# Gate matrix of a PEER layer: one-hot rows laid out for four tokens side by side instead of eight

## Chip, cores and metric

One core of a Trainium2 chip. The metric is the device time of one execution in microseconds, from the runs of the kernel; the profile is of one execution of the same program. TensorE (PE in the rows, its weight loads PEld) multiplies matrices, VectorE (DVE), ScalarE (ACT) and GpSimd (POOL) work on elements, SyncE (SP) issues most loads.

## What is computed

A diffusion backbone layer: two parallel token mixers on 1024 latent and 256 context tokens, then a PEER feed-forward part with 16384 experts of one neuron each. Only the second part is touched here. Cut to that:

```
q = (tok @ wq).reshape(-1, 8, 2, 128)
s1 = einsum("nhd,kd->nhk", q[:, :, 0], k1);  s2 = einsum("nhd,kd->nhk", q[:, :, 1], k2)
v1, i1 = top_k(s1, 16);  v2, i2 = top_k(s2, 16)
top_s, top_c = top_k((v1[..., :, None] + v2[..., None, :]).reshape(-1, 8, 256), 16)
expert = i1[top_c // 16] * 128 + i2[top_c % 16];  gate = softmax(top_s)
act = gelu(einsum("pd,ped->pe", xb, u[expert]))
out = einsum("pe,ped->pd", gate * act, v[expert])
```

Each token has 8 heads with 16 chosen experts each, so 128 slots: a first key, a second key (0 to 127 each) and a gate.

## The kernel before

The mixers come first, then norm, keys and the choice of experts. For the first 256 tokens (two blocks of 128) the rows of the chosen experts are gathered. The other 768 tokens go through all 128 expert tiles of 128 experts, and what a token has not chosen gets a gate of zero. For this a gate matrix is needed: for each token a 128 x 128 matrix over (first key, second key), with the gates at the chosen places.

`gate_block` (line 995) makes it for 32 tokens at a time. `turn` (985) has put the slots on the partitions: `rT[slot, j, token]` with the first key, the second key, and the gate as two fp16 halves that add up. `iota` holds 0 to 127, each repeated for `TB` tokens. For `TB` = 8 tokens VectorE makes the tile `oh` of shape [slot, 4, key, token] in four operations (lines 1002 to 1005): one-hot rows of the first key, one-hot rows of the second key, and these times each half of the gate. The token is the innermost dimension, so the 128 key values of one token lie 8 fp16 values, 16 bytes, apart. Then TensorE multiplies for each token the one-hot rows of the first key by the two gated rows of the second key, summed in PSUM (line 1010): the stationary operand is `oh[:, 0, :, t]` and the moving one `oh[:, 2 or 3, :, t]`, both read at that step. Four tokens (8 matmuls of 128 columns) fill one PSUM tile `pgm`, of which there is one buffer (tag `go`), and ScalarE evicts it into `gs` (line 1012). After 32 tokens `gs` is stored to `G_d`.

Six blocks of 128 tokens make 192 such groups of 8 matmuls: two blocks first, then the choice for the second half of the tokens, then four blocks. `prep` strings these steps together as a generator that yields an estimated time. For each `U_US` = 10.5 of it one early expert tile is put in: `u_turn` (transposes `put`, line 913, and the split of `uT`) and `u_act` (48 matmuls `ph` by the helper at line 99, evicted as `ac`), and two gather steps (line 892, and the product at 871 on VectorE). The framework's scheduler then settles the order of the instructions on each engine. `choosing` (scores `psc`, queries `pq`, top 16 on VectorE) and `route` (line 945 on) run between them too. All later expert tiles follow in a stage of their own, where the matmuls `pe` sum four tiles at a time.

Of the kernel before, what the change touches and what calls it, by code (L numbers as in the profile page):

```python
# [18 lines left out]
P = 128  # L19
# [12 lines left out]
# powers of two that keep the low halves of split operands out of fp16's subnormals  # L32
# [11 lines left out]
NB = 32          # tokens in a block of the gate matrix  # L44
TB = 8           # tokens whose one-hot rows are made at once
GR = 4           # expert tiles summed in PSUM at once
NGB = 2          # blocks of 128 tokens whose experts' rows are gathered
T0 = NGB * P     # the other tokens go through every expert
# [18 lines left out]
def tile_layer(ctx: ExitStack, tc: tile.TileContext, x, c, ctxt, c_ctx, ada_w, ada_b, norm_mix_g,  # L67
# [22 lines left out]
    def split(src, hi, lo, scale):  # L90
        """hi + lo = scale * src, each in fp16"""
        S.activation(hi, src, AF.Copy, scale=float(scale))  # L92
        return V.scalar_tensor_tensor(out=lo, in0=src, scalar=float(scale), in1=hi, op0=ALU.mult, op1=ALU.subtract)  # L93
# [32 lines left out]
    # activations by feature: the mixers' input first, the experts' input later  # L126
# [5 lines left out]
    def rms_cols(tiles, pl, tag):  # L132
        """1 / rms of each row of the tiles"""
        n = len(tiles)
        ss = pl.tile([P, n], F32, name=f"ss_{tag}", tag="ss", bufs=3)
        for i, t in enumerate(tiles):
            sq = pl.tile([P, D], F32, name=f"sq_{tag}{i}", tag="sq")
            S.activation(sq, t, AF.Square, accum_out=ss[:, i:i + 1])
        S.activation(ss, ss, AF.Ln, scale=1.0 / D, bias=eps)
        S.activation(ss, ss, AF.Exp, scale=-0.5)  # L140
        return ss

    def norm_T(tiles, ss, dst, sc, sh, pl, pp, tag, rows_of=None):
        """normalised rows, by feature, with a gain and a shift per feature, split in two"""
        for i, t in enumerate(tiles):
            tsc(V, t, t, ss[:, i:i + 1], ALU.mult)
        w = len(tiles) * P
        for k in range(KC):
            pt = pp.tile([P, 512], F32, name=f"pt_{tag}{k}", tag="pt", bufs=2)
            for i, t in enumerate(tiles):  # L150
                PE.transpose(pt[:, i * P:(i + 1) * P], t[:, k * P:(k + 1) * P], ident)
            hi = dst(0, k)
            S.activation(hi, pt[:, :w], AF.Identity, scale=sc(k), bias=sh(k))
            yt = pl.tile([P, 512], F32, name=f"yt_{tag}{k}", tag="yt", bufs=2)
            tsc(V, yt[:, :w], pt[:, :w], sc(k), ALU.mult, sh(k), ALU.add)
            tt(G, dst(1, k), yt[:, :w], hi, ALU.subtract)
            if rows_of is not None:
                rows_of(k, yt)
# [4 lines left out]
    # ================================================================ mixers  # L163
    with ExitStack() as mixers:
        def slab(src, c0, nm, sc, pool_lo=False):
            """128 columns of a weight, split"""
            w32 = ws.tile([P, KC, P], F32, name=f"w32_{nm}", tag="w32", bufs=3)
            ld(out=w32, in_=src[:, c0:c0 + P].rearrange("(k p) c -> p k c", p=P))
            w16 = ws.tile([P, 2, KC, P], F16, name=f"w16_{nm}", tag="w16", bufs=3)
            if pool_lo:  # L170
                tsc(G, w32, w32, float(sc), ALU.mult)
                S.copy(w16[:, 0], w32)
                tt(G, w16[:, 1], w32, w16[:, 0], ALU.subtract)
            else:
                split(w32, w16[:, 0], w16[:, 1], sc)
            return w16
# [5 lines left out]
        # ---------------------------------------------------------- modulation and norm  # L182
        with ExitStack() as sa:
# [40 lines left out]
            # lower bounds: softmax over the two layers, first entry: 1/2 + 1/2 tanh of half the difference;  # L224
            # columns: (1 + lb) / 2, (1 - lb) / 2, -(1 - lb) / 2
# [10 lines left out]
            # normalised rows by feature  # L236
# [56 lines left out]
        # tokens in three ranges: context, first half, second half  # L293
# [5 lines left out]
        def proj(w16, r, nm, pp, m=P):  # L299
            """128 columns of a projection by feature, for one range of tokens"""  # L300
            ps = pp.tile([P, 512], F32, name=f"pj_{nm}_{r}", tag="pj", bufs=2)
            o = ps[:m, :LEN[r]]
            mm3(o, lambda k: w16[:, 0, k, :], lambda k: w16[:, 1, k, :], lambda k: SRC[r][:, 0, k, :], lambda k: SRC[r][:, 1, k, :])
            return o
# [5 lines left out]
        # masks over a pair of chunks: [s, c] is kept where s and c share a chunk and s precedes c in scan order  # L310
# [18 lines left out]
        # scans restart at each chunk: zeros at the chunks' first tokens, one column early for the backward direction  # L329
# [5 lines left out]
        def v_natural(c0, nm):  # L335
            """256 value columns by token"""
# [17 lines left out]
        def gates_of(d, lf, kt, qt, esc, nm):  # L354
            """cumulates the log gates in place; queries and keys in each chunk's frame, keys by token, entry decays"""
# [49 lines left out]
        def chains(sds, v, vs, nm):  # L405
            """r[direction][position]: the state that enters a chunk, before its entry decay"""
# [30 lines left out]
        def outputs(hf, v, vs, sds, rs_, nm):  # L437
            """o by token for half of the tokens and 128 value channels, both directions"""
            po = pq.tile([P, 512], F32, name=f"o_{nm}_{hf}", tag="o", bufs=2)
            for d in range(2):  # L440
                for i in range(4):
                    p_ = hf * 4 + i
                    PE.matmul(po[:, i * P:(i + 1) * P], lhsT=scT[d][:, p_, :], rhs=v[:, 2 + p_, vs],
                              start=d == 0 and i == 0, stop=False)
            for i in range(4):
                for d in range(2):
                    for j in range(2):
                        ci = 2 * (hf * 4 + i) + j
                        PE.matmul(po[j * CH:(j + 1) * CH, i * P:(i + 1) * P], lhsT=sds[d][0][:, ci * CH:(ci + 1) * CH],
                                  rhs=rs_[d][:, ci, :], start=False, stop=i == 3 and d == 1)  # L450
            return po
# [7 lines left out]
        def head_out(v, sds, gates, gcs, ydst, nm):  # L459
            """states, outputs, head norm and gate"""  # L460
# [45 lines left out]
        def gate_tile(c0, nm):  # L506
            """z (1 + tanh(z / 2)) = 2 silu(z), up to the projection's scale"""
# [103 lines left out]
        def merge_gate(u):  # L611
            """tanh of half a merge gate, for 128 channels, kept in DRAM"""
# [8 lines left out]
        def modulation(j):  # L621
            """shift, scale or gate number j of the latent tokens: sums over the rows of ada_w, 128 of them at a time"""
# [61 lines left out]
        # ---------------------------------------------------------- merge, output projection, first half's keys  # L684
# [11 lines left out]
        def scores(hf, h, ps_pool):  # L696
            """scores of 512 tokens against both sets of keys, for one head"""
# [23 lines left out]
        def choose(hf, h, s_all, i):  # L721
            """top 16 of each key set, then of their 256 sums, for 128 tokens and one head"""
# [18 lines left out]
        def choosing(hf, ps_pool, then=None):  # L741
            """one head of half of the tokens at a time"""
# [68 lines left out]
        def h2_rows(k, yt):  # L811
            """the gathering tokens' h2 by token"""
# [43 lines left out]
    # ================================================================ PEER  # L856
# [7 lines left out]
    def gathering():  # L864
        """the chosen experts of the first tokens, a row per token at a time; rows are used AHEAD steps after their load"""
# [41 lines left out]
    def u_turn(e, un, early):  # L907
        """u of the experts i * 128 + e by feature, i on the free axis, split"""
# [16 lines left out]
    def u_act(e, uT):  # L925
        """gelu(u . h) of those experts for every token"""
# [9 lines left out]
    # product keys, gates and the gate matrix; expert tiles with e % GR == 0 go first meanwhile  # L936
    with ExitStack() as st:
# [7 lines left out]
        def route(n):  # L945
            """key numbers and gates of 128 tokens, 128 slots each"""
# [37 lines left out]
        def turn(n, sel):  # L984
            """the same as [slot, token]"""
# [9 lines left out]
        def gate_block(rT, n, nb):  # L995
            """gates of 32 tokens as [first key, second key, token]"""
            gs = pg.tile([P, P, NB], F32, name=f"gs{n}_{nb}", tag="gs", bufs=2)
            for t0 in range(0, NB, TB):
                c0 = nb * NB + t0
                oh = pg.tile([P, 4, P, TB], F16, name=f"oh{n}_{c0}", tag="oh", bufs=2)  # L1000
# [5 lines left out]
                for t1 in range(0, TB, 4):  # L1006
                    pgm = ppg.tile([P, 4, P], F32, name=f"pgm{n}_{c0}_{t1}", tag="go")
                    for t in range(4):
                        for j in (2, 3):
                            PE.matmul(pgm[:, t, :], lhsT=oh[:, 0, :, t1 + t], rhs=oh[:, j, :, t1 + t], start=j == 2, stop=j == 3)  # L1010
                    q0 = t0 + t1
                    S.activation(gs[:, :, q0:q0 + 4].rearrange("p i n -> p n i"), pgm, AF.Copy, scale=SA / SG)  # L1012
                yield 2.0
# [58 lines left out]
    # ---------------------------------------------------------- experts  # L1072
# [5 lines left out]
    def weigh(e, ac, gt4):  # L1078
        """activations times gates, split"""
# [119 lines left out]
```

## Time and profile before

| | |
|---|---|
| time, median of 3 runs | 4614.6 us (4611.57 to 4617.51) |
| profiled execution, first to last instruction | 4615.8 us |
| TensorE busy | 4416.1 us (96%) |
| VectorE busy | 2794.3 us (61%) |
| ScalarE busy | 1519.0 us (33%) |
| GpSimd busy | 1459.2 us (32%) |
| mean granted TensorE clock | 0.969 of full speed |

The profiled execution is known by its span alone, which lies within the three runs. Busy times of engines overlap each other. A busy TensorE is one that has an instruction under way, not one at its peak: what a matmul costs is read from the start of one to the start of the next. Idle time of an engine that nobody waits for costs nothing.

### The profile page before, as it was taken

The numbers are of one execution on the slowest core, as the hardware profiler recorded it, in microseconds if no ns is written. First come the engines' busy times: TensorE is split into PE (matmuls) and PEld (weight loads), VectorE is DVE, ScalarE is ACT, GpSimd is POOL, SyncE is SP. The second block draws the span as 40 slices with busy tenths as digits, with TensorE's granted clock in tenths as the row PEclk, the third lists the DMA queues.
The fourth block names the chain that finished last, engine by engine and source line by source line (L and its number), as shares of the span: only waits on it lengthen the run. The fifth ranks groups of instructions, "written<-read, shape, count | busy, mean of one in ns | idle before, by whom it ended". The sixth has DMA issues, their size and how long they took to land.

```text
span 4615.8 us, 61540 instructions
## 1 busy us (share of the span) xinstructions
PE 4416.1 (96%) x24821; PEld 2509.4 (54%) x24821; DVE 2794.3 (61%) x4946; ACT 1519.0 (33%) x2251; POOL 1459.2 (32%) x1077
## 2 busy tenths in 40 slices
PE   7999999999999989899989999999999999999998
PEld 3666566566554444455555555555555555455554
DVE  5434544334564486656985443677777776877777
ACT  6333432322332222343334433322222222222222
POOL 2111111100110345523543111444444444444442
PEclk9999999999999999799998988999999999999999
DMA  4111111101147532224433435767777776777775
GB/s 165 37 33 38 42 38 33 46 27 43 42 121 231 193 117 78 84 100 148 137 130 131 149 140 178 235 230 264 253 255 251 236 253 230 256 252 258 246 248 199
DMA packets 421019, 709.58 MB, mean 154 GB/s; under 512 B 22031, under 2 KB 286714, under 8 KB 416638
## 3 DMA queue, kind: packets, MB, share of 16 engines
q1 hardware_dynamic: 219812, 291.35, 19.4%
q0 software_dynamic: 73728, 268.47, 17.7%
q10 hardware_dynamic: 127194, 145.83, 9.3%
q8 instruction: 195, 3.19, 0.3%
q14 instruction: 90, 0.74, 0.1%
HBM read 610.14 MB, written 95.43 MB: 153 GB/s over the span
## 4 chain that ended last, share of the span: by engine, by line
PE 71%; DVE 12%; ACT 6%; DMA 4%; issue 4%; POOL 3%; ACTq 0%; SPq 0%; DVEq 0%; POOLq 0%
PE pe L99 16%; PE ph L99 15%; PE pgm L1010 8%; ACT gs L1012 3%; PE pj_f0h L99 2%; PE pv_h L99 2%; PE pv_g L99 2%; PE pj_f1h L99 2%; PE pj_m L99 2%; PE pj_qh L99 2%; PE put L913 2%; PE pj_gh L99 1%; PE pq L99 1%; PE pso L99 1%; PE pj_kg L99 1%
## 5 line engine op out<-in xcount | busy, mean ns | idle before, releaser
L99 PE MATMUL ph<-hb,uT 128*128 128x256 f16 (+1 forms) x6144 | 1094.7, 335 | 5.1 <-ACT ac L933 2.6
L99 PE MATMUL pe<-v,w 128*128 128x512 f16 x4608 | 1013.0, 380 | 18.9 <-DVE acc L1102 13.3
L99 PEld LDWEIGHTS <-uT 128*128 128x128 f16 x6144 | 619.3, 101 | 409.4 <-issue 34.1
L99 PEld LDWEIGHTS <-w 128*128 128x128 f16 x4608 | 451.2, 98 | 567.3 <-issue 20.0
L920 POOL TENSOR_TENSOR uT<-uf,uT 128x512 f16<-128x512 f32 x256 | 361.0, 1420 | 476.1 <-ACT uf L919 474.2
L892 POOL DMA_INDIRECT row_False<-in_peer_u_dram,idx x256 | 303.2, 1185 | 459.1 <-DVE row_False L871 410.2
L892 POOL DMA_INDIRECT row_True<-in_peer_v_dram,idx x256 | 296.7, 1159 | 452.1 <-DVE gacc L876 406.3
L871 DVE SCALAR_TENSOR_TENSOR row_False<-row_False,h2n 128x1024 f32<-128x1024 f32 x256 | 345.0, 1354 | 139.0 <-DMA row_False<-in_peer_u_dram,idx 139.0
L1010 PE MATMUL pgm<-oh 128*128 128x128 f16 x1536 | 391.2, 410 | 37.9 <-ACT gs L1012 31.2
L876 DVE SCALAR_TENSOR_TENSOR gacc<-row_True,dots,gacc 128x1024 f32<-128x1024 f32 x254 | 356.2, 1402 | 1.6
L88 DVE TENSOR_TENSOR oh<-iota,rTr 128x1024 f16<-128x1024 f16 x192 | 151.8, 827 | 325.8 <-PE pgm L1010 325.8
L1012 ACT ACTIVATE gs<-pgm 128x512 f32<-128x512 f32 x192 | 204.8, 1067 | 419.0 <-PE pgm L1010 418.9
L1010 PEld LDWEIGHTS <-oh 128*128 128x128 f16 x1536 | 223.5, 146 | 179.0 <-issue 64.2
L933 ACT ACTIVATE ac<-ph 128x256 f32<-128x256 f32 (+1 forms) x256 | 125.3, 494 | 441.2 <-PE ph L99 434.1
L1102 DVE TENSOR_TENSOR acc<-pe,acc 128x512 f32<-128x512 f32 x372 | 252.9, 686 | 15.1 <-PE pe L99 15.0
L92 ACT ACTIVATE v<-vn 128x1024 f16<-128x1024 f32 x128 | 135.0, 1057 | 337.9 <-DMA vn<-in_peer_v_dram 222.5
L917 ACT ACTIVATE uT<-put 128x512 f16<-128x512 f32 x256 | 153.5, 600 | 272.3 <-PE put L913 264.2
L93 DVE SCALAR_TENSOR_TENSOR v<-vn,v 128x1024 f16<-128x1024 f32 x128 | 177.2, 1392 | 72.9 <-ACT v L92 68.5
L99 PE MATMUL pj_m<-hb,w_m 128*128 128x512 f16 x768 | 186.1, 399 | 2.2 <-DVE lf_g L85 1.6
L99 PE MATMUL pq<-hb,w_wq 128*128 128x512 f16 x768 | 180.7, 384 | 4.5 <-POOL w_wq L88 3.0
L99 PEld LDWEIGHTS <-hb 128*128 128x128 f16 x1536 | 150.3, 98 | 17.3
L919 ACT ACTIVATE uf<-put 128x512 f32<-128x512 f32 x256 | 154.9, 605 | 11.8 <-issue 7.6
(360 smaller groups left out, 5948.0 us busy)
## 6 DMA issues: line engine op xcount, KB each, us to landing
un<-in_peer_u_dram SPq DMA_DIRECT2D x128, 512.0 KB
vn<-in_peer_v_dram SPq DMA_DIRECT2D x128, 512.0 KB
G_d<-gs ACTq DMA_DIRECT2D x24, 2048.0 KB
gt<-G_d ACTq DMA_DIRECT2D x32, 1536.0 KB
act_d<-ac ACTq DMA_DIRECT2D x48, 384.0 KB
acr<-act_d SPq DMA_DIRECT2D x48, 384.0 KB
mw<-in_ada_w_dram SPq DMA_DIRECT2D x32, 512.0 KB
w_wq<-in_peer_wq_dram SPq DMA_DIRECT2D x32, 512.0 KB
```

What stands on the lines that cost most here:

```text
L88: eng.tensor_tensor(out=out, in0=in0, in1=in1, op=op)
L93: return V.scalar_tensor_tensor(out=lo, in0=src, scalar=float(scale), in1=hi, op0=ALU.mult, op1=ALU.subtract)
L99: PE.matmul(ps, lhsT=a(k), rhs=b(k), start=n == 0, stop=n == last)
L871: V.scalar_tensor_tensor(out=row, in0=row, scalar=1.0, in1=h2n, op0=ALU.mult, op1=ALU.mult, accum_out=dots[:, s:s + 1])
L876: V.scalar_tensor_tensor(out=gacc[n], in0=row, scalar=dots[:, s:s + 1], in1=gacc[n], op0=ALU.mult, op1=ALU.add)
L892: G.indirect_dma_start(out=row, out_offset=None, in_=src[0], in_offset=bass.IndirectOffsetOnAxis(ap=gsel[n][0][:, s:s + 1], axis=0))
L917: S.activation(hi, pv, AF.Copy, scale=SU)
L919: S.activation(uf, pv, AF.Copy, scale=SU)
L920: pace[0] = G.tensor_tensor(out=lo, in0=uf, in1=hi, op=ALU.subtract)
L1010: PE.matmul(pgm[:, t, :], lhsT=oh[:, 0, :, t1 + t], rhs=oh[:, j, :, t1 + t], start=j == 2, stop=j == 3)
L1012: S.activation(gs[:, :, q0:q0 + 4].rearrange("p i n -> p n i"), pgm, AF.Copy, scale=SA / SG)
L1102: vmark[0] = V.tensor_tensor(out=acc[n][:, hs], in0=ps, in1=acc[n][:, hs], op=ALU.add)
```

## The change

`TB` becomes 4. A tile `oh` then holds the rows of four tokens, a key's values lie 4 fp16 values, 8 bytes, apart, and four tiles are allocated instead of two. A tile is now just what one PSUM group needs, so the loop over `t1` goes away; a step yields 1.0 for four tokens where it yielded 2.0 for eight. (The changed file has no comments; line numbers after 1006 differ by up to two.)

```diff
-TB = 8           # tokens whose one-hot rows are made at once
+TB = 4
...
-                oh = pg.tile([P, 4, P, TB], F16, name=f"oh{n}_{c0}", tag="oh", bufs=2)
+                oh = pg.tile([P, 4, P, TB], F16, name=f"oh{n}_{c0}", tag="oh", bufs=4)
...
-                for t1 in range(0, TB, 4):
-                    pgm = ppg.tile([P, 4, P], F32, name=f"pgm{n}_{c0}_{t1}", tag="go")
-                    for t in range(4):
-                        for j in (2, 3):
-                            PE.matmul(pgm[:, t, :], lhsT=oh[:, 0, :, t1 + t], rhs=oh[:, j, :, t1 + t], start=j == 2, stop=j == 3)
-                    q0 = t0 + t1
-                    S.activation(gs[:, :, q0:q0 + 4].rearrange("p i n -> p n i"), pgm, AF.Copy, scale=SA / SG)
-                yield 2.0
+                pgm = ppg.tile([P, TB, P], F32, name=f"pgm{n}_{c0}", tag="go")
+                for t in range(TB):
+                    for j in (2, 3):
+                        PE.matmul(pgm[:, t, :], lhsT=oh[:, 0, :, t], rhs=oh[:, j, :, t], start=j == 2, stop=j == 3)
+                S.activation(gs[:, :, t0:t0 + TB].rearrange("p i n -> p n i"), pgm, AF.Copy, scale=SA / SG)
+                yield 1.0
```

On VectorE, in block 6, from token 24 on, the order before (`oh6_24` is the tile that begins with token 24; the rows at line 871 are gather products):

```order
L88 TENSOR_TENSOR oh6_24_20093<-iota_14450,rTr6_19932 128x1024 x2
L1004 TENSOR_TENSOR oh6_24_20093<-oh6_24_20093,rTr6_19932 128x1024
L88 TENSOR_TENSOR oh6_24_20093<-oh6_24_20093,rTr6_19932 128x1024
L871 SCALAR_TENSOR_TENSOR row0_38_False_19847,dots0_16201<-row0_38_False_19847,h2n0_16199 128x1024
L871 SCALAR_TENSOR_TENSOR row0_39_False_19850,dots0_16201<-row0_39_False_19850,h2n0_16199 128x1024
L88 TENSOR_TENSOR oh6_32_20227<-iota_14450,rTr6_19932 128x1024 x2
L88 TENSOR_TENSOR oh6_40_20252<-iota_14450,rTr6_19932 128x1024
```

And at the same tokens after the change:

```order
L88 TENSOR_TENSOR oh6_24_20428<-iota_14450,rTr6_20252 128x512 x2
L1004 TENSOR_TENSOR oh6_24_20428<-oh6_24_20428,rTr6_20252 128x512
L88 TENSOR_TENSOR oh6_24_20428<-oh6_24_20428,rTr6_20252 128x512
L88 TENSOR_TENSOR oh6_28_20443<-iota_14450,rTr6_20252 128x512 x2
L1004 TENSOR_TENSOR oh6_28_20443<-oh6_28_20443,rTr6_20252 128x512
L88 TENSOR_TENSOR oh6_28_20443<-oh6_28_20443,rTr6_20252 128x512
L871 SCALAR_TENSOR_TENSOR row0_38_False_20137,dots0_16361<-row0_38_False_20137,h2n0_16359 128x1024
L871 SCALAR_TENSOR_TENSOR row0_39_False_20140,dots0_16361<-row0_39_False_20140,h2n0_16359 128x1024
L88 TENSOR_TENSOR oh6_32_20567<-iota_14450,rTr6_20252 128x512 x2
L88 TENSOR_TENSOR oh6_36_20582<-iota_14450,rTr6_20252 128x512
```

Four operations of 1024 elements have become eight of 512; the two gather products stand between the same tokens, 31 and 32.

On TensorE, in block 6, where the group of tokens 40 to 43 ends and the next begins, the order before (`put` are transposes of an expert tile):

```order
L1010 LDWEIGHTS oh6_40_20252
L1010 MATMUL pgm6_40_0_20257<-oh6_40_20252 128x128
L913 MATMUL put96_0_21356<-ident_60,un96_21353 128x128 x4
L913 MATMUL put96_1_21365<-ident_60,un96_21353 128x128 x3
L1010 LDWEIGHTS oh6_40_20252
L1010 MATMUL pgm6_40_4_20267<-oh6_40_20252 128x128
```

And after the change (the pair at line 99 stands there five times; one is shown, and the pairs of the groups likewise):

```order
L1009 LDWEIGHTS oh6_40_20597
L1009 MATMUL pgm6_40_20602<-oh6_40_20597 128x128
...
L99 LDWEIGHTS uT92_21708
L99 MATMUL ph1_92_21881<-hb1_83,uT92_21708 128x512
...
L1009 LDWEIGHTS oh6_44_20612
L1009 MATMUL pgm6_44_20617<-oh6_44_20612 128x128
```

Each group now reads a tile of its own, and the expert work between two groups is another piece of it. Over the program the groups are still 192 of 8 matmuls, mostly with four `ph` between them, and the work between the first two blocks and the last four differs by no more than eight `pq` and one `ph`.

## Rows read from the trace of the kernel before

**Rows 1.** The page: span, busy time, chain that ended last by engine and line.
```profile
span 4615.8 us, 61540 instructions
...
PE 4416.1 (96%) x24821; PEld 2509.4 (54%) x24821; DVE 2794.3 (61%) x4946; ACT 1519.0 (33%) x2251; POOL 1459.2 (32%) x1077
...
PE 71%; DVE 12%; ACT 6%; DMA 4%; issue 4%; POOL 3%; ACTq 0%; SPq 0%; DVEq 0%; POOLq 0%
PE pe L99 16%; PE ph L99 15%; PE pgm L1010 8%; ACT gs L1012 3%; PE pj_f0h L99 2%; PE pv_h L99 2%; PE pv_g L99 2%; PE pj_f1h L99 2%; PE pj_m L99 2%; PE pj_qh L99 2%; PE put L913 2%; PE pj_gh L99 1%; PE pq L99 1%; PE pso L99 1%; PE pj_kg L99 1%
```

**Rows 2.** Busy by stretch: length, PE, PEld, DVE, ACT, POOL, granted clock, DMA, GB/s.
```profile
1916.00:2192.00 276.00, 261.03 (x1243) 155.59 (x1241) 172.98 (x403) 109.11 (x147) 88.29 (x54) 0.89 0.32 118
2192.00:2340.00 148.00, 142.42 (x828) 83.20 (x826) 138.67 (x592) 47.78 (x85) 83.36 (x72) 1.00 0.41 134
2340.00:2850.00 510.00, 480.61 (x2327) 294.50 (x2328) 259.31 (x405) 206.22 (x282) 129.60 (x89) 0.90 0.37 135
2860.00:4600.00 1740.00, 1718.53 (x9232) 913.76 (x9231) 1273.17 (x1458) 485.59 (x769) 775.62 (x622) 1.00 0.74 246
```

**Rows 3.** Instructions of tile `oh`: duration ns (min/median/max), first and last start.
```profile
L1010 PEld LDWEIGHTS <-oh x1536: 140/145/170, 1919.1 to 2848.3; 128*128 128x128 f16 x192
L1010 PE MATMUL pgm<-oh x1536: 384/412/432, 1923.9 to 2848.5; 128*128 128x128 f16 x192
```

**Rows 4.** Busy time by stretch, instructions of tile `oh` alone: PE, PEld, DVE.
```profile
1916.00:2192.00 276.00, 129.93 (x512) 74.79 (x512) 102.78 (x128) 0.89 0.32 118
2340.00:2850.00 510.00, 261.28 (x1024) 148.74 (x1024) 195.49 (x256) 0.90 0.37 135
```

**Rows 5.** Waits, 1916 to 2850: total us, times, longest.
```profile
PE pgm L1010 <- ACT gs L1012: 31.2, 100, 0.7
...
DVE oh L88 <- PE pgm L1010: 325.8, 85, 11.2
```

**Rows 6.** Timeline from 2613.2: start us, length us, engine, instruction, count, idle before.
```profile
2613.30 2.01 PE L1010 MATMUL pgm<-oh 128*128 128x128 f16 x8
...
2615.14 1.04 PE L99 MATMUL ph<-hb,uT 128*128 128x512 f16 x4
2615.35 1.08 ACT L1012 ACTIVATE gs<-pgm 128x512 f32<-128x512 f32 x1 [1.19 <-PE pgm L1010]
...
2616.48 0.39 PE L1010 MATMUL pgm<-oh 128*128 128x128 f16 x1 [0.30 <-ACT gs L1012]
```

**Rows 7.** Timeline of PE, 2604 to 2607.
```profile
2604.54 2.57 PE L99 MATMUL ph<-hb,uT 128*128 128x256 f16 x22
2606.94 0.39 PE L1010 MATMUL pgm<-oh 128*128 128x128 f16 x1
```

**Rows 8.** Timeline of PE, 2050 to 2053.
```profile
2050.56 2.04 PE L1010 MATMUL pgm<-oh 128*128 128x128 f16 x8
2052.42 1.03 PE L99 MATMUL ph<-hb,uT 128*128 128x512 f16 x2
```

**Rows 9.** Busy time by stretch, two short stretches; the clock is the third from last.
```profile
2042.00:2055.00 13.00, 13.00 (x44) 6.17 (x43) 5.17 (x8) 4.41 (x5) 0.05 (x1) 0.50 0.34 141
2610.00:2628.00 18.00, 16.65 (x71) 9.36 (x71) 8.78 (x13) 7.44 (x11) 5.25 (x4) 1.00 0.24 81
```

**Rows 10.** Timeline of PE, 2627.6 to 2629.
```profile
2627.85 1.05 PE L913 MATMUL put<-ident,un 128*128 128x128 f32 x8
2628.74 0.49 PE L99 MATMUL ph<-hb,uT 128*128 128x256 f16 x3
```

**Rows 11.** Timeline of DVE, 2599 to 2601.
```profile
2600.01 0.68 DVE L88 TENSOR_TENSOR oh<-oh,rTr 128x1024 f16<-128x1024 f16 x1
2600.62 1.22 DVE L871 SCALAR_TENSOR_TENSOR row_False<-row_False,h2n 128x1024 f32<-128x1024 f32 x1
```

**Rows 12.** Timeline of DVE, 2006 to 2007.2.
```profile
2006.62 0.41 DVE L88 TENSOR_TENSOR eqr<-eqr 128x512 f16<-128x512 f16 x1
2006.95 0.68 DVE L1004 TENSOR_TENSOR oh<-oh,rTr 128x1024 f16<-128x1024 f16 x1
```

## The prediction, made before the changed kernel was run

> **What bounds the kernel now.** I read the page first, for the engine that carries the end: TensorE is busy for 96% of the span and for 71% of the chain that ended last, and `pgm`, the matmuls that build the gate matrix from one-hot rows, hold 8% of that chain by themselves, their eviction `gs` another 3% [rows 1]. Then the busy time by stretch [rows 2]: the gate matrix is made in two stretches of 276 us (two blocks of 128 tokens, 64 groups of 8 matmuls) and 510 us (four blocks, 128 groups). TensorE is busy for 261 and 481 us of them, VectorE for 173 and 259. Between them lies a stretch in which routing has VectorE busy for 139 of 148 us, and behind them the expert tiles, where TensorE works for 1718.5 of 1740 us. So time taken from TensorE in the two gate stretches comes off the end, unless another engine there has no room: nothing later waits for it.
>
> The matmuls in question are 1536 [rows 3], and inside the two stretches their busy time is 129.9 + 261.3 us [rows 4]. The view of waits says who is late: VectorE waits 325.8 us for `pgm` to release a one-hot tile, while TensorE waits 31.2 us for the eviction, 100 times, 0.7 us at most [rows 5]. TensorE is the slow side of the one-hot tiles.
>
> One period shows how [rows 6]. Eight `pgm` matmuls start at 2613.30, the next instruction on TensorE (`ph`, expert work) at 2615.14: 1.84 us, **0.230 us a matmul**. Four `ph` (0.86 us, 1.04 less a drain of 0.18) fill the time in which ScalarE evicts (2615.35, 1.08 us); TensorE then stands for 0.30 us, and the next group starts at 2616.48. The period is 3.18 us: 1.84 of matmuls, 0.2 of drain, 1.08 of eviction and some 0.05 of signalling. There is one PSUM buffer for the groups, so matmuls and eviction of successive groups cannot overlap; the four `ph` are what fits between.
>
> What does 0.230 us consist of? A 256-column matmul, twice as wide, with a weight load of its own and packed operands, goes every 0.109 us (22 from 2604.54 to 2606.94) [rows 7]. The array is therefore not the limit. And the rate does not follow TensorE's clock: at 2050.56, with a granted clock of 0.50, eight `pgm` take 1.86 us, 0.233 each, where the stretch from 2610 at 1.00 gave 0.230 [rows 6, 8, 9]. What limits them is how operands come from memory. Both operands are read at a step of 8 fp16 values, 16 bytes. The weight load is no candidate: its median is 145 ns [rows 3], below 230.
>
> **The change part by part.** *Step of 8 bytes instead of 16, 1536 matmuls.* No row shows an fp16 operand at 8 bytes, so I bound it. Above: 0.231 as now, no gain. I exclude a loss, since the elements lie closer and nothing is added to the read. Below: half of the packed 256-column price, 0.055 us. The nearest row is the 128-column fp32 transpose with its own weight load, 8 from 2627.85 to 2628.74, 0.111 us [rows 10]. Since the price is not set by the array clock, I take it to go with the memory passed over: 128 elements now span 2 KB a partition, then 1 KB. That gives half of 0.231, **0.116 us**, close to the transpose row. Saving: 1536 x (0.231 - 0.116) = **177 us**; ends 0 and 1536 x 0.176 = 270 us. [...]
>
> *Does all of it arrive?* The period becomes 0.93 + 0.2 + 1.08 + 0.05 = 2.26 us, TensorE's work in it 0.93 + 0.86 = 1.79, so it still stands about 0.4 us for the eviction, as now: the cut is one for one. Where 5 or more other matmuls separate two groups, TensorE is the bound alone, and it is one for one again. The stretches become 276 - 64 x 0.92 = 217 and 510 - 128 x 0.92 = 392 us.
>
> *VectorE: 768 instructions on 512 elements in place of 384 on 1024.* These take 0.61 us from start to start now, 0.68 each in duration (from 2600.01 to 2600.62) [rows 11]. A 512-element fp16 operation takes 0.41, and its successor starts after 0.33 [rows 12]. So a group costs 1.3 to 1.64 us instead of 1.2 to 1.4. I take 1.64: 64 x 1.64 = 105 us and 128 x 1.64 = 210 us, where they hold 102.8 and 195.5 now [rows 4]. With the 70 and 64 us of other VectorE work (the difference to rows 2) that is 175 of 217 and 274 of 392 us. TensorE's shortened work still covers it: **nothing**. If the cover were gone, it would be the case of the half-speed rows below.
>
> *Tiles, waits, queues.* Four tiles of four tokens are in flight, as were two of eight: the same 16 tokens and the same memory. VectorE now waits for TensorE once per group, not once per two. Behind that wait stand the other `oh` operations, routing and gather products, in the order in which they stood before; a release comes after one group, so this wait gets shorter. The orders show that routing and gathers keep their places between the tokens, so the middle stretch is as before. Evictions stay at 192 of 1.07 us, stores of `gs` and all DMAs keep their number and size on SP's, ScalarE's and GpSimd's queues, only nearer together: 118 and 135 GB/s in the stretches now, where the expert stage moves 246 [rows 2]. Eviction becomes the next late one. ScalarE's other work there fits into the gaps: its busy share is 40% of both stretches. Nothing.
>
> *Clock.* The granted clock is 0.89 and 0.90 in the two stretches and 1.00 in the middle and after [rows 2]; it is at 0.50 from 2042 to 2055 [rows 9], behind runs of `pgm`. Less time in slowly fed matmuls may end such falls; `ph` at half clock loses. At half clock for 22% and 20% of the stretches means 163 us, of which `ph` holds about half (four would take 1.72 us beside 1.86 of `pgm`), so that 40 us at most could come back. A loss would need more half clock with the same columns in less time; I count 0 and keep -40 to +15 for the range.
>
> **Sum.** 177 + 0 + 0 + 0. The profiled execution has a span of 4615.8 us, 1.2 above the median of the three runs shown, so on the scale of the runs 4614.6 - 177 = **4438 us**.
>
> **The rivals.** (a) *Full speed at 8 bytes.* Then 0.055 us a matmul: 270 us off, stretches of 186 and 330 us against VectorE's 175 and 274, just covered: **4345**. For it: the price is memory, not array. Against it: at 16 bytes the price is over four times that of packed columns, more than one step of two. [...]
>
> (b) *VectorE becomes the bound.* Runs of four values rather than eight could take away the double rate of the 16-bit operations. A 512-element operation would then cost 0.69 us, about what a long one does now: 64 x 2.76 + 70 = 247 us and 128 x 2.76 + 64 = 417, that is 30 and 25 us over the shortened stretches. The gain falls to 122: **4493**. For it: the tokens are the innermost dimension, and the key column is read with a zero step outside it. Against it: with runs of eight these operations go at 1024 in 0.61 us, as fast as operations on 16-bit data without such a broadcast, so the broadcast costs nothing now.
>
> (c) *The same, worse: slower.* If a four-value run costs a restart, the price could be 1.0 us for 512 elements. VectorE then needs 64 x 4 + 70 = 326 and 128 x 4 + 64 = 576 us, 50 and 66 more than the stretches have: **4731**. It decides from (276 - 70) / 256 = 0.80 us in the first stretch and (510 - 64) / 512 = 0.87 in the second, above the price of today's operations with twice the elements. Little speaks for it.
>
> (d) *The step does nothing.* If the price hangs on reading apart at all, or on the weights and columns being read at once, 0.231 stays, VectorE's work stays hidden and the time is **4615**. [...]
>
> **How the numbers follow.** Forecast 0.60, (a) 0.15, (b) 0.11, (d) 0.08, (c) 0.04, anything else 0.02. A measurement of this kernel can tell about 0.2%, 9 us, from no change. Faster by more: forecast, (a), (b), a little of the rest: 0.87. Within: most of (d): 0.07. Slower: (c), and (d) with some stalls added: 0.06. The forecast's own range, with the clock and a matmul between 0.105 and 0.13 us, is 4395 to 4475. The range reaches on to (a) and (b) and leaves (c) and (d) out: 4340 to 4500.
>
> **What would show it.** Right: `pgm` starts 0.11 to 0.12 us apart at both clock levels, evictions 2.25 us apart in a run, the stretches 217 and 392 us, short `oh` operations of at most 0.41 us, VectorE still waiting for `pgm`. The forecast is wrong if the spacing of `pgm` is near 0.055 or stays at 0.23, or if TensorE waits for `oh` for tens of microseconds instead of for `gs`; then (a), (d) or (b) holds.

## The result, and the profile after

| | before | after |
|---|---|---|
| median | 4616.06 us (4 runs) | 4441.15 us (4 runs, 4436.34 to 4443.93) |
| ratio to before | | 0.9616, interval 0.9602 to 0.9629 |
| span of the profiled execution | 4615.8 us | 4440.5 us |

The change saves 175 us; 177 were forecast, and 4441 lies 3 us above the 4438 of the prediction. The page of the kernel after, the lines that answer to rows 1:

```profile
PE 4211.8 (95%) x24821; PEld 2448.8 (55%) x24821; DVE 2837.0 (64%) x5330; ACT 1518.1 (34%) x2253; POOL 1468.8 (33%) x1077
...
PE pe L99 16%; PE ph L99 14%; PE pgm L1009 3%; PE pv_g L99 2%; PE pv_h L99 2%; PE pj_f1h L99 2%; DVE oh L88 2%; PE pj_f0h L99 2%; PE pj_m L99 2%; PE pj_qh L99 2%; ACT gs L1010 2%; PE put L913 2%; PE pq L99 1%; POOL row_False L892 1%; DVE row_False L871 1%
```

The gate matmuls fell from 8% of the chain that ended last to 3%, their eviction from 3% to 2%, and VectorE's one-hot operations, which the list of rows 1 does not name, stand in it with 2%.

Busy time by stretch, cut at the same events as rows 2 (the engines as there: PE, PEld, DVE, ACT, POOL, then granted clock):

```profile
1916.00:2132.00 216.00, 194.52 (x1267) 137.20 (x1268) 184.62 (x526) 113.17 (x155) 94.05 (x54) 0.97 0.41 152
2132.00:2279.00 147.00, 142.15 (x814) 82.07 (x811) 132.89 (x591) 46.31 (x83) 81.69 (x71) 0.99 0.41 133
2279.00:2674.00 395.00, 346.31 (x2334) 254.00 (x2335) 298.58 (x669) 205.99 (x284) 138.38 (x89) 0.97 0.48 175
2684.00:4424.00 1740.00, 1717.83 (x9221) 912.63 (x9220) 1269.06 (x1457) 482.90 (x767) 775.52 (x622) 1.00 0.74 246
```

The two gate stretches are 216 and 395 us long where 217 and 392 were forecast; the middle and the expert stage are as before. All of the gain lies in these two. The instructions of `oh` alone in them (PE, PEld, DVE; compare rows 4):

```profile
1916.00:2132.00 216.00, 71.03 (x512) 58.33 (x512) 120.35 (x256) 0.97 0.41 152
2279.00:2674.00 395.00, 141.98 (x1024) 116.46 (x1024) 221.62 (x512) 0.97 0.48 175
```

TensorE spends 213 us on them instead of 391: 178 us less. VectorE spends 342 us instead of 298, which is 1.78 us for each of the 192 groups. One period, in the timeline around 2436 (start us, length us):

```profile
2435.74 1.10 PE L1009 MATMUL pgm<-oh 128*128 128x128 f16 x8
...
2436.66 1.26 PE L99 MATMUL ph<-hb,uT 128*128 128x512 f16 x5
2436.88 1.07 ACT L1010 ACTIVATE gs<-pgm 128x512 f32<-128x512 f32 x1 [1.19 <-PE pgm L1009]
...
2438.00 1.10 PE L1009 MATMUL pgm<-oh 128*128 128x128 f16 x8
```

From 2435.74 to 2436.66 are 0.92 us for eight matmuls, **0.115 us** each where rows 6 have 0.230, and the period is 2438.00 - 2435.74 = 2.26 us, as forecast to the hundredth. The same at a granted clock of 0.50, first the stretch, then TensorE's timeline in it:

```profile
2330.20:2336.80 6.60, 4.53 (x22) 2.75 (x23) 6.60 (x18) 2.55 (x4) 2.43 (x3) 0.50 0.41 146
```

```profile
2335.06 1.13 PE L1009 MATMUL pgm<-oh 128*128 128x128 f16 x8
2336.01 1.44 PE L99 MATMUL ph<-hb,uT 128*128 128x512 f16 x4
```

0.95 / 8 = 0.119 us, beside 0.115 at a granted clock of 1.00 (2434 to 2440). As in rows 8, this price does not follow the clock. TensorE's waits in the two stretches and between them (total us, times, longest; compare rows 5):

```profile
PE pgm L1009 <- ACT gs L1010: 28.2, 93, 1.4
PE pstr L989 <- DVE selr L88: 15.8, 3, 7.9
PE ph L99 <- POOL uT L920: 10.8, 3, 4.3
PE pgm L1009 <- DVE oh L1004: 8.6, 5, 4.0
PE pgm L1009 <- DVE oh L88: 7.8, 20, 1.8
```

The same waits before, from 1916 to 2850, beside the eviction's 31.2 us in rows 5:

```profile
PE pstr L989 <- DVE selr L88: 9.5, 2, 8.4
PE pgm L1010 <- DVE oh L1004: 4.4, 1, 4.4
PE ph L99 <- POOL uT L920: 1.9, 1, 1.9
...
PE pgm L1010 <- DVE oh L88: 0.2, 1, 0.2
```

The wait for the eviction stays, at 28 us. The waits for one-hot rows that are not ready grow from 4.6 to 16.4 us. VectorE in turn waits less for TensorE than the 325.8 us of rows 5, so most of its reserve is used up:

```profile
DVE oh L88 <- PE pgm L1009: 98.6, 84, 5.9
```

### The profile page after: what moved, and what is told of

It is laid out like the page before. It is cut to its first block, busy times and chain, and to the rows that moved or that the text cites. A ratio compares the mean times of both kernels' runs of the same rounds, so it can differ in the third digit from the quotient of the medians.

```text
span 4440.5 us, 61921 instructions
## 1 busy us (share of the span) xinstructions
PE 4211.8 (95%) x24821; PEld 2448.8 (55%) x24821; DVE 2837.0 (64%) x5330; ACT 1518.1 (34%) x2253; POOL 1468.8 (33%) x1077
## 4 chain that ended last, share of the span: by engine, by line
PE 65%; DVE 15%; issue 6%; ACT 5%; DMA 4%; POOL 4%; ACTq 0%; SPq 0%; POOLq 0%; DVEq 0%
PE pe L99 16%; PE ph L99 14%; PE pgm L1009 3%; PE pv_g L99 2%; PE pv_h L99 2%; PE pj_f1h L99 2%; DVE oh L88 2%; PE pj_f0h L99 2%; PE pj_m L99 2%; PE pj_qh L99 2%; ACT gs L1010 2%; PE put L913 2%; PE pq L99 1%; POOL row_False L892 1%; DVE row_False L871 1%
## 5 line engine op out<-in xcount | busy, mean ns | idle before, releaser
L99 PE MATMUL ph<-hb,uT 128*128 128x256 f16 (+1 forms) x6144 | 1063.8, 329 | 12.0 <-POOL uT L920 11.7
L99 PEld LDWEIGHTS <-uT 128*128 128x128 f16 x6144 | 609.2, 99 | 371.5 <-issue 15.1
L1009 PE MATMUL pgm<-oh 128*128 128x128 f16 x1536 | 213.0, 295 | 47.7 <-ACT gs L1010 28.2
L88 DVE TENSOR_TENSOR oh<-iota,rTr 128x512 f16<-128x512 f16 x384 | 188.7, 527 | 98.9 <-PE pgm L1009 98.6
L1009 PEld LDWEIGHTS <-oh 128*128 128x128 f16 x1536 | 174.8, 116 | 98.3 <-issue 73.5
L1081 ACT CAST w<-ac 128x768 f16<-128x768 f32 x80 | 66.5, 832 | 275.1 <-DVE ac L88 275.1
```

What stands on the lines that cost most here:

```text
L88: eng.tensor_tensor(out=out, in0=in0, in1=in1, op=op)
L99: PE.matmul(ps, lhsT=a(k), rhs=b(k), start=n == 0, stop=n == last)
L1009: PE.matmul(pgm[:, t, :], lhsT=oh[:, 0, :, t], rhs=oh[:, j, :, t], start=j == 2, stop=j == 3)
```

## Experiments

Theory M: the step in memory at which the operands are read sets the price of a gate matmul, and that price alone explains the gain. Rival T: the smaller tiles and operations, released one by one, are what helps. The code is cut to the lines that matter; `iota` and the key columns follow the layout.

**The step alone.** Tiles, operations and release as before; only the order inside a tile differs.

```diff
-oh = pg.tile([P, 4, P, TB], F16, ...)
+oh = pg.tile([P, 4, 2, P, 4], F16, ...)
...
-PE.matmul(..., lhsT=oh[:, 0, :, t1 + t], rhs=oh[:, j, :, t1 + t], ...)
+PE.matmul(..., lhsT=oh[:, 0, a, :, b], rhs=oh[:, j, a, :, b], ...)   # a, b = divmod(t1 + t, 4)
```

> The step alone: two tiles of eight tokens and VectorE operations of 1024 elements as before, but inside a tile the tokens lie as two blocks of four, so that both operands are read at a step of 8 bytes. Theory M (the step in memory sets the price of a gate matmul): matmuls start 0.118 us apart, evictions 2.25 us apart in a run, time 4430 to 4450 us, VectorE busy about 20 us less than in the change. Rival T (the gain came from smaller tiles that are released one by one): 0.23 us apart, 4605 to 4625 us.

Measured: 4451.05 us, ratio 0.9632, interval 0.9612 to 0.9652, which overlaps that of the change; the median lies 1 us above the expected range. TensorE's timeline:

```profile
2438.00 1.10 PE L1014 MATMUL pgm<-oh 128*128 128x128 f16 x8 [0.28 <-ACT gs L1016]
2438.92 1.26 PE L100 MATMUL ph<-hb,uT 128*128 128x512 f16 x5
```

Again 0.92 us for eight. M holds: 171 us come without the smaller tiles. VectorE's total is 2816.1 us, 21 less than with the change, as expected. The 10 us by which the median lies above the change are not in the gate stretches: the last gate matmul starts at 2674.5 us in this kernel and at 2672.9 in the change, the spans end at 4452.1 and 4440.5. Of the difference behind it TensorE's waits for the expert sums (13.3 us in the change, 19.5 here) are a part; the rest I did not trace.

**The operations alone.** Tiles of eight tokens at 16 bytes, but made in two halves by eight operations of 512 elements.

```diff
+for h in range(0, TB, 4):
+    w = slice(h, h + 4)
-    tt(V, oh[:, 0], iota, col(0), ALU.is_equal)
+    tt(V, oh[:, 0, :, w], iota[:, :, 0:4], col(0), ALU.is_equal)
```

> The rest without the step: tiles of eight tokens at 16 bytes, made by eight VectorE operations of 512 elements, four tokens at a time. Theory M: matmuls 0.23 us apart, 4605 to 4625 us. Rival T (finer VectorE work is what helps): below 4560 us.

Measured: 4609.9 us in one run (before: 4622.27 over 7 runs, 4613.78 to 4629.56). TensorE's timeline:

```profile
2437.42 2.02 PE L1012 MATMUL pgm<-oh 128*128 128x128 f16 x8 [0.28 <-ACT gs L1014]
2439.27 1.04 PE L99 MATMUL ph<-hb,uT 128*128 128x512 f16 x4
```

1.85 / 8 = 0.231 us. T falls as the account of the gain: this run lies only 12 us below the median of before and 4 us below its fastest run, with a higher mean granted clock (0.979; under *Clock* below). This is the half of the change that costs VectorE something, without the half that pays for it. The four tiles in flight were not tried at 16 bytes; at eight tokens a tile they would take twice the memory.

**Which operand.** Two kernels with the stationary operand (one-hot rows of the first key) in a tile of its own: first 16 bytes for the stationary and 8 for the moving operands, then the reverse.

```diff
+oa = pg.tile([P, P, TB], F16, ...);  oh = pg.tile([P, 3, 2, P, 4], F16, ...)
...
+oa = pg.tile([P, 2, P, 4], F16, ...);  oh = pg.tile([P, 3, P, TB], F16, ...)
```

> Stationary operand at 16 bytes, moving operands at 8, tile size and operation count as before. Theory M with the moving operand as the slow read: 0.118 us a matmul, 4430 to 4450 us. M with both reads adding up: about 0.175 us, 4520 to 4540 us. M with the weight load as the slow read: 0.23 us, 4605 to 4625 us.

> The reverse: stationary operand at 8 bytes, moving operands at 16. Moving operand as the slow read: 0.21 to 0.23 us a matmul, 4590 to 4625 us. Both reads adding up: about 0.175 us, 4520 to 4540 us. Weight load as the slow read: 0.118 us, 4430 to 4450 us.

Measured: 4452.02 (2 us above the range) and 4611.07 us, one run each. TensorE's timeline of the first, then of the second:

```profile
2436.97 1.13 PE L1013 MATMUL pgm<-oh,oa 128*128 128x128 f16 x8 [0.30 <-ACT gs L1015]
2437.92 1.26 PE L99 MATMUL ph<-hb,uT 128*128 128x512 f16 x5
```

```profile
2437.76 1.99 PE L1013 MATMUL pgm<-oh,oa 128*128 128x128 f16 x8
2439.57 1.04 PE L99 MATMUL ph<-hb,uT 128*128 128x512 f16 x4
```

0.95 / 8 = 0.119 and 1.81 / 8 = 0.226 us. The moving operand sets the price; the step of the weights moves it by some 0.004 (0.119 beside 0.115, 0.226 beside 0.230). The reads do not add up, for which 0.175 was expected.

**Smaller steps.** Four blocks of two tokens in a tile of eight (4 bytes), then the key innermost (2 bytes, packed).

```diff
+oh = pg.tile([P, 4, 4, P, 2], F16, ...)
...
+oh = pg.tile([P, 4, TB, P], F16, ...)
+col = lambda j: rT[:, j, c0:c0 + TB].unsqueeze(2).to_broadcast([P, TB, P])
```

> As the run with the step alone, but four blocks of two tokens: a step of 4 bytes. If the price of a matmul goes with the memory passed over (16, 8, 4 bytes), it halves again to 0.06 us, evictions come 1.8 us apart and the time is 4355 to 4390 us, provided VectorE keeps its rate with runs of two values (0.69 us per 1024 elements). If 8 bytes were already at a floor, 0.11 to 0.118 us and 4440 to 4455. If VectorE loses its double rate (1.2 us per 1024), TensorE waits for the one-hot tiles for tens of us and the time is 4430 to 4480 whatever the matmuls cost.

> Key innermost: operands packed, step 2 bytes, the token's key broadcast along the innermost dimension on VectorE. The matmul's price is then that of packed columns: 0.055 us by half of the 256-column row. VectorE reads a value with step zero: if it loses the double rate, 1.2 us per 1024 elements, 2.4 us per group, VectorE is the bound and the time is 4430 to 4490; if not, 4345 to 4390.

Measured: 4394.65 us, ratio 0.9502, interval 0.9486 to 0.9518, for 4 bytes, just above the expected range; 4514.56 us in one run for the packed rows, above what was expected too. TensorE's timeline at 4 bytes, one whole period, and with packed rows:

```profile
2400.58 0.62 PE L1014 MATMUL pgm<-oh 128*128 128x128 f16 x8 [0.39 <-ACT gs L1016]
2401.03 1.02 PE L100 MATMUL ph<-hb,uT 128*128 128x512 f16 x4
2402.35 0.62 PE L1014 MATMUL pgm<-oh 128*128 128x128 f16 x8 [0.29 <-ACT gs L1016]
```

```profile
2436.76 0.61 PE L1012 MATMUL pgm<-oh 128*128 128x128 f16 x8 [0.49 <-ACT gs L1014]
2437.21 1.03 PE L100 MATMUL ph<-hb,uT 128*128 128x512 f16 x4
```

At 4 bytes 0.45 / 8 = 0.056 us, halved once more, and a period of 1.77 us. Packed rows cost 0.056 us too, so that the price does not halve again from 4 to 2 bytes. But TensorE now waits for VectorE, at 4 bytes:

```profile
PE pgm L1014 <- ACT gs L1016: 44.4, 117, 2.9
PE pgm L1014 <- DVE oh L1007: 25.8, 13, 5.5
PE pgm L1014 <- DVE oh L89: 9.8, 13, 1.9
```

and with packed rows:

```profile
PE pgm L1012 <- DVE oh L1006: 67.5, 30, 7.1
```

The operations behind this, first at 4 bytes, then packed, in VectorE's timeline:

```profile
2402.56 0.69 DVE L1007 TENSOR_TENSOR oh<-oh,rTr 128x1024 f16<-128x1024 f16 x1
```

```profile
2442.64 1.22 DVE L1006 TENSOR_TENSOR oh<-oh,rTr 128x1024 f16<-128x1024 f16 x1
```

With runs of two values VectorE keeps its rate (0.69 us per 1024 elements). With one key value repeated along the innermost dimension it takes 1.22 us, and most of what the cheaper matmuls would give is lost behind it: rival (b) of the prediction, in another layout.

**Two PSUM buffers** for the groups, in the change and in the kernel with 4 bytes.

```diff
-pgm = ppg.tile([P, TB, P], F32, name=f"pgm{n}_{c0}", tag="go")
+pgm = ppg.tile([P, TB, P], F32, name=f"pgm{n}_{c0}", tag="go", bufs=2)
```

> The change with two PSUM buffers for the groups. If the chain of matmuls, eviction and next matmuls is what is left (period 2.26 us against 1.8 of TensorE work), TensorE's 28 us of waits for the eviction go and the time is 4405 to 4425. If VectorE or the order of the instructions takes its place, 4430 to 4445.

> Step of 4 bytes and two PSUM buffers. If both terms hold, TensorE's work alone is left: 1536 matmuls at 0.06 and no wait for the eviction, 4320 to 4350 us; if VectorE is the bound with runs of two, the same time as the step of 4 bytes with one buffer.

Measured: 4430.03 us (4416.67 to 4442.23), ratio 0.9576, interval 0.9548 to 0.9604, and 4396.14 us, ratio 0.9507, interval 0.9491 to 0.9523. The first overlaps the change's interval by a little, the second is that of one buffer. TensorE's waits in the first:

```profile
PE pgm L1009 <- DVE oh L1004: 25.3, 11, 9.2
PE ph L99 <- POOL uT L920: 22.7, 6, 7.8
...
PE pgm L1009 <- DVE oh L88: 6.1, 5, 2.6
PE pgm L1009 <- ACT gs L1010: 3.4, 8, 1.0
```

The wait for the eviction goes from 28.2 to 3.4 us, and the waits for VectorE's `oh` and GpSimd's `uT` grow from 27.2 together to 54.1. The chain of matmuls and eviction is real, and most of what is freed there goes into these waits. But the order on TensorE is another as well: the last gate matmul starts at 2594.7 us instead of 2672.9, and 384 more `ph`, the work of eight expert tiles, come behind it (4416 instead of 4032). So the kernel differs from the change by more than a buffer, and what the eviction alone costs is not shown.

**Small tiles and small step together**, beside the change itself on the same chip.

```diff
-oh = pg.tile([P, 4, P, TB], F16, name=f"oh{n}_{c0}", tag="oh", bufs=4)
+oh = pg.tile([P, 4, 2, P, 2], F16, name=f"oh{n}_{c0}", tag="oh", bufs=4)
```

> The change with each tile of four tokens split into two blocks of two, a step of 4 bytes, four tiles in flight. Matmuls 0.057 us apart as with the step of 4 bytes and tiles of eight. If releasing tile by tile matters, 4375 to 4390 us; if VectorE's 768 shorter operations (0.41 us) make it later, 4395 to 4410 us.

> The change itself, beside the run before it on the same chip: 4436 to 4446 us, matmuls 0.118 us apart.

Measured: **4384.81 us**, ratio 0.9476, interval 0.9458 to 0.9493, and 4442.42 us, ratio 0.9602, interval 0.9586 to 0.9619, for the change. It has the lowest median of all versions. Its interval lies clear of the change's and overlaps a little that of tiles of eight at 4 bytes (0.9486 to 0.9518), which was measured on another chip. TensorE's timeline, across a rise of the granted clock, with the two stretches:

```profile
2402.17 1.01 PE L1014 MATMUL pgm<-oh 128*128 128x128 f16 x8
2403.02 1.25 PE L100 MATMUL ph<-hb,uT 128*128 128x256 f16 x10
2404.34 0.62 PE L1014 MATMUL pgm<-oh 128*128 128x128 f16 x8
2404.80 1.03 PE L100 MATMUL ph<-hb,uT 128*128 128x256 f16 x6
```

```profile
2396.40:2402.40 6.00, 5.43 (x35) 4.58 (x36) 3.52 (x10) 3.01 (x4) 0.00 (x0) 0.50 0.27 101
2403.50:2406.00 2.50, 2.26 (x22) 1.58 (x20) 2.46 (x7) 2.50 (x5) 1.21 (x1) 1.00 0.00 1
```

At the lower level eight matmuls take 0.85 us (0.106 each; 0.86 for the eight from 2397.45 to 2398.31, which lie wholly in the stretch at 0.50), at the higher 0.46 (0.058). At a step of 4 bytes the price follows the clock, as it did not at 16 and 8: the array's rate is now the limit, to go by these two levels alone. The 10 us against tiles of eight are, as with the step alone, not in the gate stretches (the last gate matmul starts at 2618.2 us here, at 2613.6 there).

## Why the prediction was right

*The step, 177 us.* Right, mechanism and size: 0.116 us forecast, 0.115 measured; 178 us less TensorE time on these matmuls. The two reasons for taking half were that the price did not follow the clock and that it should go with the memory passed over. Both were tested: 0.231, 0.115 and 0.056 us for 16, 8 and 4 bytes. What the prediction left open, which operand it is, the pair of kernels settled: the moving one. Whether it is the memory passed over or the number of values in a given length of it that counts, these steps cannot tell apart, for the one doubles when the other halves.

*One for one.* Right: stretches of 216 and 395 us, period 2.26 us, TensorE standing for the eviction as before.

*VectorE: nothing.* Not quite. Most operations cost what was taken (0.42 us, at 2435.75 below, against 0.41):

```profile
2435.75 0.42 DVE L88 TENSOR_TENSOR oh<-oh,rTr 128x512 f16<-128x512 f16 x1
```

But the longest takes 3.87 us, and a group 1.78 us in the mean where 1.64 were taken: 342 us in place of 315. Summed over a stretch the cover looked whole, in the forecast (274 of 392 us) and in the trace (299 of 395). Single places, where routing or a gather product stands ahead of `oh`, had none: the longest wait for `oh`, 3.96 us up to 2332.03, stands behind a gather product of 4.66 us that starts at 2323.53. TensorE's idle time in the two stretches grew from 44 us (786 - 741.6) to 70 us (611 - 540.8). Of these 26 us the waits for `oh` are 12 (4.6 to 16.3), those for `selr`, VectorE's routing, 7 (8.4 to 15.8), and those for `uT` 7 (none to 6.7).

*Clock: 0.* Wrong by about as much, the other way. The granted clock in the stretches rose from 0.89 and 0.90 to 0.97, and TensorE's other work there shrank from 350 to 328 us (741.6 - 391.2 and 540.8 - 213.0). That is within the 40 us named as the bound. So the balance is 178 + 23 - 26 = 175 us: two terms set to nothing cancelled each other, and that the forecast came within 3 us is in this part luck. That the clock rose *because* of the faster matmuls is not shown: no run changed the clock alone, and one run speaks against it. The kernel with the operations alone has its matmuls at 0.231 us and yet a mean granted clock of 0.979 over its one run, above the 0.969 to 0.975 of the seven runs of before beside it and near the 0.981 of the profiled run after the change. From 1916 us to the last gate matmul, before has 0.91 (to 2849) with 492 us of other TensorE work, and the change 0.97 (to 2673) with 469 us.

*The rivals.* (a), full speed at 8 bytes, is out: a step of 8 bytes brings half the price of 16, 0.115 us, and only 4 bytes bring 0.056. (d) is out with it. (b) did not happen in the change (0.42 us per 512 elements) and did in the packed layout (1.22 us per 1024). (c) has no support in any run.

## What to carry to other kernels

When a narrow matmul's start-to-start time exceeds that of a wider one and does not change with the granted clock, look at the step of its moving operand: here 16, 8 and 4 bytes cost 0.231, 0.115 and 0.056 us per 128 columns, while the step of the weights hardly counted (0.119 us with the weights at 16 bytes, 0.115 with them at 8). Let the innermost run of tokens be as short as the engine that writes the operand allows: VectorE kept its rate down to runs of two (0.69 us per 1024 elements) and lost it with a repeated value innermost (1.22). And when an engine's cover is checked by sums over a stretch, also check the places where its other work stands ahead of what the bound engine needs.

## Not expected

- Of the steps tried, the limit changes hands at 4 bytes: 0.057 us at full clock is both a quarter of the price at 16 bytes and what packed operands reach (0.056), but at a granted clock of 0.50 it is 0.106, where 8 bytes cost 0.119 (0.115 at full clock) and 16 bytes 0.233 (0.230).
- The weight load gets shorter with the step as well (medians of 145, 116 and 97 ns for 16, 8 and 4 bytes), but it does not set the price: at 4 bytes it takes 97 ns and the matmuls start 0.056 us apart, and with only the weights at 16 bytes they start 0.119 us apart. So the prediction's reason for ruling it out, 145 ns being less than 230, does not carry; the pair of kernels settles it.
- VectorE's rate did not care whether runs were eight, four or two values long: medians of 0.69 us per 1024 elements for each.
- With four tiles of four instead of two of eight the median is some 10 us lower at either step, none of it in the gate stretches. The kernels ran on different chips or at different times and their intervals overlap, so the gain is not sure, and why is open.
